# One-core hybrid decoder layer: output strips split two ahead, VectorE's order written out for the first SwiGLU strips, stores on GpSimd's queue, way down in blocks of 3, 4, 4

## The chip, the cores and the metric

The kernel runs on one core of one Trainium2 chip. The metric is device time in microseconds (us), the median of several runs; lower is better. All data is float32 and the matmuls run on float32r operands.

## What is computed

A decoder layer on x of shape (1, 1024, 1024): three mixing branches (gated linear attention, forgetting attention, cross-attention into 256 memory tokens), each projected to 1024 channels, gated and summed, then an output projection with a residual, then a SwiGLU feed-forward layer with another residual. The change touches only the end of it:

```
merged = sum_i gates_i * (y_i @ w_branch[i])
x = x + merged @ w_out
h2 = rmsnorm(x, g_ffn)
x = x + (silu(h2 @ w_ffn_gate) * (h2 @ w_ffn_up)) @ w_ffn_down      # D_FF = 2816
```

## The kernel before, in words

Everything is kept transposed, channels on the 128 partitions and the 1024 tokens along the free axis, in two halves of 512 (`H2`). A float32 operand is split into a high part (ScalarE casts it, L912) and a low part (VectorE subtracts, L913); one product is three matmuls, high·high, high·low, low·high (`mm3`, L844, L846, L848), each 128x128 by 128x512 into one of 8 PSUM banks. The split of a 128x1024 weight strip needs a slot of three rings: `w4` (raw, 6 slots), `h4` and `l4` (high and low, 3 slots each).

- **Output projection** (`out_half`, L923). Two halves of the tokens, 8 strips each; a strip is 24 matmuls. Per strip: load x (L929), load and split a `w_out` strip (L934, L935), the matmuls, the residual add (L940), the store of the new x to DRAM (L941, `x_d`), the square and its sum for the norm. `half_factors` turns the sum into the norm's factors, a broadcast by a matmul with ones (L959), copied to a `w4` tile `rb` (L961). In the second half, after strip 1, eight multiplies (L989) and eight splits (`hop`) make the operands `B11` and `B21` of the first half.
- **SwiGLU in pairs of strips** (L1111 to L1163). The 22 column blocks of gate and up go in 11 pairs; a pair's gate and up are each a 2x2 block product in Strassen-Winograd form, 7 products (`SEQ`, L1000) of 4 steps of `mm3`: 168 matmuls a pair. The weight-side sums are made in `strips` (L1018) from two loads `ra` (L1022) and `rb_` (L1023); the token-side operands (`B11`, `B21`, `T2`, `T1`, `T3`, `B22`, `T4`) are made once, in the first pair (L1129 to L1148), and kept. The first two products need no sums; so PE's order runs those of gate 0, up 0 and gate 1 ahead (their strips are split by `early`, L969), and the other five follow. An intermediate result is read from a PSUM bank while the bank goes on accumulating, by ScalarE (`keep`, L1054) or VectorE (`plus`, L907): the product after next on that bank waits for the read.
- **Stores and sums in passing.** `Pair.store` (L1083) writes the seven operands of the way down to DRAM (`act_d`, L1091). `down_sums` (L1093) loads the down weights of a pair into two `w4` tiles, makes four sums and stores them (`sum_d`, L1104).
- **Way down** (`down`, L1181). Blocks of 3, 3, 3, 2 pairs (`DOWN`, L30); per block four column pairs `jj`, each again 7 products, now of as many steps as the block has pairs. `down_ops` (L1170) loads a pair's seven operands through four `w4` tiles and splits them.

PE's order is the program's (`manual_schedule`, L142). All other engines and the queue of DMA issues on SyncE (SP), on which every DMA is, are put in order by a scheduler that simulates the program's times; once built, each queue is strictly in that order.

Of the kernel before, what the change touches and what calls it, by code (L numbers as in the profile page):

```python
# [12 lines left out]
F32 = mybir.dt.float32  # L13
F32R = mybir.dt.float32r
# [63 lines left out]
def trunk(tc, xT, memT, wT, wmkv, wmq0, wmq1, wgv, wfox, a2, par, cst, wbr, wout, wfg, wfu, wfd, outT):  # L78
# [841 lines left out]
    hops = {}  # L920
    gain = lambda k: pr[:, C_GFFN + k:C_GFFN + k + 1]

    def out_half(h):  # L923

        sl = H2[h]
        ssq = ws.tile([P, 512], F32, tag="l2", bufs=2, name="ssq")
        for j in range(KT):
            x1[j][h] = x = cell("x1")
            nc.sync.dma_start(x, xT[j][:, sl])  # L929
            if h == j == 0:  # L930
                hi, lo = wout0
            else:
                raw = w4()
                nc.sync.dma_start(raw, wout[j])  # L934
                hi, lo = split(h4(), l4(), raw)  # L935
# [33 lines left out]
    def early(src):  # L969
# [3 lines left out]
        return split(ep.tile([P, S], F32R, tag="eh", bufs=2, name="eh"),  # L973
                     ep.tile([P, S], F32R, tag="el", bufs=2, name="el"), raw)

    for ssq in out_half(0):
        if ssq is not None and x1[1][0] is None:
            W0.close()
            E = ExitStack()
            ep = pool(E, "early")  # L980
    fac = half_factors(ssq)
    for j, ssq in enumerate(out_half(1)):
        if j == 0:
            next(fac)
        if j == 1:
            rb = next(fac)
            for k in range(KT):
                x = x1[k][0]
                nc.vector.scalar_tensor_tensor(x, x, gain(k), rb, ALU.mult, ALU.mult)  # L989
                hops["B11" if k < 4 else "B21", k % 4] = hop(hp1, "ha", 8, x)  # L990
        x = x1[j][1]
        nc.scalar.activation(x, x, AF.Copy, scale=gain(j))
        if j > 3:
            sub(x, x, x1[j - 4][1])
    fac = half_factors(ssq)

# [18 lines left out]
                    reads[i](ps)  # L1015
                yield

    def strips(src, first=None):  # L1018

        ra, rb_, sa, sb = w4(), w4(), w4(), w4()  # L1020
        lo_, hi_ = slice(0, 512), slice(512, 1024)
        nc.sync.dma_start(ra, src[:, 0:S])  # L1022
        nc.sync.dma_start(rb_, src[:, S:2 * S])  # L1023
        s2, s1, s3, s4 = sa[:, lo_], sa[:, hi_], sb[:, lo_], sb[:, hi_]
        a = first or split(h4(), l4(), ra)
        add(s1, rb_[:, lo_], rb_[:, hi_])
        sub(s2, s1, ra[:, lo_])
        b = split(h4(), l4(), sa)
        sub(s4, ra[:, hi_], s2)
        sub(s3, ra[:, lo_], rb_[:, lo_])  # L1030
        c = split(h4(), l4(), sb)
        d = split(h2(), l2(), rb_[:, hi_])
        at_ = {"A11": (*a, 0), "A12": (*a, 512), "S2": (*b, 0), "S1": (*b, 512), "S3": (*c, 0), "S4": (*c, 512),
               "A22": (*d, 0)}
# [5 lines left out]
        return get  # L1040

    hB = lambda name, k: hops[name, k]

    class Pair:
# [38 lines left out]
        def store(self, p):  # L1083
            (b11, b12), (b21, b22) = self.u
            t1, t2, t3, t4 = (cell("T") for i in range(4))
            sub(t1, b12, b11)
            sub(t2, b22, t1)
            sub(t3, b22, b12)
            sub(t4, b21, t2)
            for i, t in enumerate((b11, b21, t2, t1, t3, b22, t4)):  # L1090
                nc.sync.dma_start(act_d[p][i], t)  # L1091

    def down_sums(p):  # L1093

        ta, tb = w4(), w4()
        a11, a12, a22, a21 = d = [t[:, s] for t in (ta, tb) for s in H2]
        for o in range(4):
            nc.sync.dma_start(d[o].rearrange("p (j c) -> p j c", c=P), wfd[:, p, :, o, :].rearrange("j p c -> p j c"))
        add(a22, a21, a22)
        sub(a21, a11, a21)  # L1100
        sub(a11, a22, a11)
        sub(a12, a12, a11)
        for o, t in enumerate((a11, a22, a21, a12)):
            nc.sync.dma_start(sum_d[p][:, :, o, :].rearrange("j p c -> p j c"), t.rearrange("p (j c) -> p j c", c=P))  # L1104

    def go(gen, n=99):
        for _ in zip(range(n), gen):
            pass


    pairs = [Pair(), Pair()]  # L1111
    wg0 = strips(wfg[0])
    e1, e2 = early(wfu[0]), early(wfg[1])
    lazy = {}
    late = lambda nm, src, e: lambda name, k: tuple(t[:, (name == "A12") * 512 + k * P:(name == "A12") * 512 + k * P + P]
                                                    for t in e) if name in ("A11", "A12") else lazy[nm](name, k)
    q0, q1, q2 = pairs[0].gate(wg0), pairs[0].up(late("u0", wfu[0], e1)), pairs[1].gate(late("g1", wfg[1], e2))
    go(q0, 4)
    next(fac)
    go(q0, 4)  # L1120
    go(q1, 2)
    rb = next(fac)
    go(q1, 6)
    go(q2, 8)
    E.close()
    BM.close()
    hp2 = pool(root, "h2b")

    for k in range(4):  # L1129
        t3, t2 = x1[k + 4][1], w4()[:, :512]  # L1130
        mul(t3, t3, rb)
        add(t2, t3, x1[k][0])
        hops["T2", k] = hop(hp2, "hb", 20, t2)
        sub(x1[k + 4][0], x1[k + 4][0], t2)
    lazy["u0"] = strips(wfu[0], e1)
    for k in range(4):
        b12, t1 = x1[k][1], x1[k][0]
        mul(b12, b12, rb)
        sub(t1, b12, t1)
        hops["T1", k] = hop(hp2, "hb", 20, t1)  # L1140
    for k in range(4):
        hops["T3", k] = hop(hp2, "hb", 20, x1[k + 4][1])
    for k in range(4):
        b22 = x1[k][1]
        add(b22, x1[k + 4][1], b22)
        hops["B22", k] = hop(hp2, "hb", 20, b22)
    for k in range(4):
        hops["T4", k] = hop(hp2, "hb", 20, x1[k + 4][0])  # L1148
    for i in range(5):
        go(q0, 4)  # L1150
        go(q1, 4)
    pairs[0].store(0)
    lazy["g1"] = strips(wfg[1], e2)
    for p in range(1, NP):
        q = q2 if p == 1 else Pair.gate(pair := Pair(), strips(wfg[p]))
        if p == 1:
# [2 lines left out]
        if p == 4:  # L1159
            down_sums(0)  # L1160
        go(q)
        go(pair.up(strips(wfu[p])))
        pair.store(p)  # L1163


    ORDER = ("B11", "B21", "T2", "T1", "T3", "B22", "T4")
    acc = [[None, None] for j in range(KT)]
    ops = {}

    def down_ops(p):  # L1170

        for i in range(0, 7, 2):
            w = min(2, 7 - i)
            raw = w4()
            nc.sync.dma_start(raw[:, :w * 512].rearrange("p (o c) -> p o c", c=512),
                              act_d[p][i:i + w].rearrange("o p c -> p o c"))
            for o in range(w):
                t = (hp1, "ha", 8) if i == 0 else (hp2, "hb", 20)
                ops[ORDER[i + o], p] = hop(*t, raw[:, o * 512:(o + 1) * 512])

    def down(b, p0, n):  # L1181
        first, last = b == 0, p0 + n == NP
        for q in range(n):
            if (ORDER[0], p0 + q) not in ops:
                down_ops(p0 + q)
        for jj in range(4):
            if jj == 2 and not last:
                down_ops(p0 + n)
# [41 lines left out]
            go(products(get, lambda name, k: ops[name, p0 + k], n, reads))  # L1230

    p0 = 0
    for b, n in enumerate(DOWN):
# [72 lines left out]
```

## Time and profile before

| | us |
|---|---|
| median of 3 runs | 1727.69 (1725.42 to 1728.51) |
| profiled execution, own time | 1728.52 |
| its span, first to last instruction | 1726.7 |
| PE busy | 1672.0 (97%) |
| VectorE (DVE) busy | 992.7 (57%) |
| ScalarE (ACT) busy | 643.4 (37%) |
| GpSimd (POOL) busy | 101.6 (6%) |

The output projection ends at about 1030 us of the span, the SwiGLU pairs at about 1490, the way down at the end. A busy PE is not yet a PE at its rate: each stretch also has a count of matmuls and a granted clock (1.00 is 2.4 GHz, 0.5 is 1.2 GHz), and the three are read together. Engines wait in order: what stands at the head of an engine's queue holds back all behind it.

### The profile page before, as it was taken

To read this page: it belongs to the slowest core of one execution; us is meant where nothing else is said; L and a number is where in the kernel's file an instruction comes from. 1 tells how busy PE (TensorE), PEld (TensorE's weight loads), DVE (VectorE), ACT (ScalarE), POOL (GpSimd) and SP (SyncE) were. 2 spreads that over 40 slices of the span, in tenths; PEclk is the share of its full clock that TensorE was granted. 3 is DMA by queue.
4 is the path that set the end of the run, shared out by engine and by line. 5 is a ranking of instruction groups with operands and counts; after the bars stand their busy time and mean duration, and the time that the engine had idled before them with its cause. 6 is when DMAs were issued, how large, how long until landed. Compare 5 with 4: busy or idle time off the path is not lost.

```text
span 1726.7 us, 21934 instructions
## 1 busy us (share of the span) xinstructions
PE 1672.0 (97%) x8411; PEld 1401.4 (81%) x8411; DVE 992.7 (57%) x1581; ACT 643.4 (37%) x1096; POOL 101.6 (6%) x88
## 2 busy tenths in 40 slices
PE   8999999999999999999999896999999999898999
PEld 7889988878789999988887674877778878686787
DVE  8435554342435565554465468666766665757766
ACT  6334544232224444443123344333333333642421
POOL 2000100000001000000252000000000000000000
PEclk9999999999999999999999997999999999999999
DMA  6441221111231122127546322545545445847633
GB/s 232 134 125 56 68 75 51 62 61 49 62 95 55 62 65 65 50 80 246 195 160 219 115 93 74 182 140 184 162 152 173 141 145 167 264 147 252 209 117 135
DMA packets 152586, 220.79 MB, mean 128 GB/s; under 512 B 11153, under 2 KB 93601, under 8 KB 152481
## 3 DMA queue, kind: packets, MB, share of 16 engines
q1 hardware_dynamic: 152480, 219.39, 39.2%
q8 instruction: 66, 1.08, 0.3%
q14 instruction: 40, 0.32, 0.1%
HBM read 160.30 MB, written 59.05 MB: 127 GB/s over the span
## 4 chain that ended last, share of the span: by engine, by line
PE 85%; DVE 6%; DMA 5%; ACT 2%; issue 1%; SPq 0%; POOL 0%; DVEq 0%; ACTq 0%
PE ps L844 14%; PE ps L848 14%; PE ps L846 14%; PE pt L157 5%; PE pt L159 4%; PE pt L158 4%; PE pm L236 4%; PE pm L238 4%; PE pm L237 4%; PE pm L199 2%; PE pm L203 2%; PE pm L201 2%; DMA w<-in_wfd 2%; DVE hbl L913 1%; DMA w<-in_wfu 1%
## 5 line engine op out<-in xcount | busy, mean ns | idle before, releaser
L844 PE MATMUL ps<-hbh,h 128*128 128x512 f32 x660 | 265.5, 402 | 29.9 <-ACT h L912 12.2
L846 PE MATMUL ps<-hbl,h 128*128 128x512 f32 x660 | 265.0, 402 | 4.3 <-DVE hbl L913 4.3
L848 PE MATMUL ps<-hbh,l 128*128 128x512 f32 x660 | 266.1, 403 | 0.0
L912 ACT CAST h<-w 128x1024 fp32r<-128x1024 f32 (+4 forms) x165 | 141.7, 860 | 329.9 <-PE ps L846 271.8
L913 DVE TENSOR_TENSOR l<-w,h 128x1024 fp32r<-128x1024 f32 (+4 forms) x165 | 162.1, 985 | 60.5 <-ACT h L912 60.2
L844 PEld LDWEIGHTS ps<-hbh,h 128*128 128x128 f32 x660 | 126.7, 192 | 66.4 <-ACT h L912 14.0
L236 PE MATMUL pm<-whi,hh 128*128 128x384 f32 (+2 forms) x512 | 162.3, 317 | 0.0
L238 PE MATMUL pm<-whi,hl 128*128 128x384 f32 (+2 forms) x512 | 159.0, 310 | 0.0
L237 PE MATMUL pm<-wlo,hh 128*128 128x384 f32 (+2 forms) x512 | 158.9, 310 | 0.0
L846 PEld LDWEIGHTS ps<-hbl,h 128*128 128x128 f32 x660 | 126.7, 192 | 35.6 <-DVE hbl L913 4.9
L848 PEld LDWEIGHTS ps<-hbh,l 128*128 128x128 f32 x660 | 126.4, 192 | 30.6 <-DVE l L913 0.8
L157 PE MATMUL pt<-hh,whi 128*128 128x512 f32 x352 | 142.3, 404 | 0.0
L159 PE MATMUL pt<-hh,wlo 128*128 128x512 f32 x352 | 138.1, 392 | 0.0
L158 PE MATMUL pt<-hl,whi 128*128 128x512 f32 x352 | 138.1, 392 | 0.0
L236 PEld LDWEIGHTS pm<-whi,hh 128*128 128x128 f32 x512 | 96.4, 188 | 2.6
L237 PEld LDWEIGHTS pm<-wlo,hh 128*128 128x128 f32 x512 | 96.4, 188 | 2.5
L848 PE MATMUL ps<-hah,l 128*128 128x512 f32 x248 | 96.7, 390 | 1.1 <-DVE l L913 1.1
L846 PE MATMUL ps<-hal,h 128*128 128x512 f32 x248 | 97.1, 392 | 0.0
L844 PE MATMUL ps<-hah,h 128*128 128x512 f32 x248 | 97.0, 391 | 0.0
L238 PEld LDWEIGHTS pm<-whi,hl 128*128 128x128 f32 x512 | 96.3, 188 | 0.0
L189 DVE TENSOR_TENSOR wlo<-raw,whi 128x512 fp32r<-128x512 f32 (+2 forms) x64 | 50.6, 792 | 77.5 <-ACT whi L188 76.9
L907 DVE TENSOR_TENSOR acc<-ps,acc 128x512 f32<-128x512 f32 x96 | 66.2, 690 | 46.0 <-PE ps L848 44.7
(319 smaller groups left out, 3124.3 us busy)
## 6 DMA issues: line engine op xcount, KB each, us to landing
w<-act_d SPq DMA_DIRECT2D x33, 512.0 KB, 4.2
tg<-tg_d SPq DMA_DIRECT2D x24, 512.0 KB, 3.5
w<-in_wfd SPq DMA_DIRECT2D x48, 256.0 KB, 3.3
w<-in_wfg SPq DMA_DIRECT2D x23, 512.0 KB, 4.2
w<-in_wfu SPq DMA_DIRECT2D x23, 512.0 KB, 4.3
raw<-in_wT SPq DMA_DIRECT2D x22, 512.0 KB, 4.2
tg_d<-gz SPq DMA_DIRECT2D x22, 512.0 KB, 2.9
sum_d<-w SPq DMA_DIRECT2D x44, 256.0 KB, 3.0
```

The source lines that it names most:

```text
L157: nc.tensor.matmul(ps, hi[:, ks], hh[k][:, sl], start=k == 0, stop=False)
L158: nc.tensor.matmul(ps, hi[:, ks], hl[k][:, sl], start=False, stop=False)
L159: nc.tensor.matmul(ps, lo[:, ks], hh[k][:, sl], start=False, stop=k == KT - 1)
L236: nc.tensor.matmul(ps[:, :n], hh[k][:, ms], hi, start=k == 0, stop=False)
L237: nc.tensor.matmul(ps[:, :n], hh[k][:, ms], lo, start=False, stop=False)
L238: nc.tensor.matmul(ps[:, :n], hl[k][:, ms], hi, start=False, stop=k == KT - 1)
L844: nc.tensor.matmul(ps, hi, a, start=first, stop=False, skip_group_check=more)
L846: nc.tensor.matmul(ps, hi, b, start=False, stop=False, skip_group_check=more)
L848: nc.tensor.matmul(ps, lo, a, start=False, stop=last, skip_group_check=more)
L907: add = lambda o, a, b: nc.vector.tensor_tensor(o, a, b, ALU.add)
L912: nc.scalar.copy(hi, raw)
L913: nc.vector.tensor_tensor(lo, raw, hi.bitcast(F32), ALU.subtract)
```

## The change

Six edits; the core of the diff:

```diff
-DOWN = (3, 3, 3, 2)
+DOWN = (3, 4, 4)
 # output projection: strips split two ahead; x_d stored from GpSimd's queue
+    wo = {0: wout0}
+    def out_w(i):
+        if i < 2 * KT:
+            raw = w4()
+            nc.sync.dma_start(raw, wout[i % KT])
+            wo[i] = split(h4(), l4(), raw)
+    out_w(1)
...
-            if h == j == 0: hi, lo = wout0
-            else: raw = w4(); nc.sync.dma_start(raw, wout[j]); hi, lo = split(h4(), l4(), raw)
+            out_w(h * KT + j + 2)
+            hi, lo = wo.pop(h * KT + j)
...
-            nc.sync.dma_start(x_d[j][h], x)
+            nc.gpsimd.dma_start(x_d[j][h], x)
 # half_factors: the factors stay in PSUM
-        rb = w4()[:, :512]
-        nc.scalar.copy(rb, ps)
-        yield rb
+        yield ps
 # second half: B11, B21 two a strip; first parts of up 0, gate 1, gate 0 in strips 4, 5, 6
-            for k in range(KT):
+        if 1 <= j <= 4:
+            for k in (2 * j - 2, 2 * j - 1):
                 x = x1[k][0]
                 nc.vector.scalar_tensor_tensor(x, x, gain(k), rb, ALU.mult, ALU.mult)
                 hops["B11" if k < 4 else "B21", k % 4] = hop(hp1, "ha", 8, x)
+        if j == 4: e1 = early(wfu[0])
+        if j == 5: e2 = early(wfg[1])
+        if j == 6: parts_g0 = strip_parts(wfg[0], at_0); next(parts_g0)
...
+    BM.close()                       # before: after E.close(), behind gate 1's first two products
+    hp2 = pool(root, "h2b")          # 16 slots of "hb" (20 before); T4 has a pool of its own, opened after E.close()
 # stores of the way down's operands and sums
-                nc.sync.dma_start(act_d[p][i], t)
+                nc.gpsimd.dma_start(act_d[p][i], t)
...
-            nc.sync.dma_start(sum_d[p]..., t...)
+            nc.gpsimd.dma_start(sum_d[p]..., t...)
 # first pair: VectorE in program order too
+    ve = tc.manual_schedule(engines={mybir.EngineType.DVE})
+    ve.__enter__()
     go(q0, 4); next(fac); go(q0, 4); rb = next(fac)
+    staggered("T2", t2_sum)          # per k: product and sum, cast on ScalarE, then the low part of k - 1
+    go(q1, 8)
+    u0 = strip_parts(wfu[0], at_u, e1); go(u0, 2)          # S2, S1 of up 0
+    staggered("T1", t1_sum)
     go(q2, 8); E.close()
+    go(q0, 4); go(q1, 4); staggered("T3", ...); next(u0)
+    go(q0, 4); go(q1, 4); staggered("B22", b22_sum, lambda: next(u0))
+    go(q0, 4); go(q1, 4); staggered("T4", t4_sum)
+    go(q0, 4); go(q1, 4); g1 = strip_parts(wfg[1], at_g, e2); go(g1, 2)
+    go(q0, 4); go(q1, 4); next(g1); next(g1)
+    ve.__exit__(None, None, None)
 # way down: an operand is loaded into its own low tile and split in place
+    def feed():                      # for each wanted operand, as soon as its ring has a free slot
+                hi = pl.tile(...); lo = pl.tile(...)
+                nc.sync.dma_start(lo.bitcast(F32), act_d[p][ORDER.index(name)])
+                raw.append((x, hi, lo))
+    def need(p0, n): wanted.extend(...); feed()
+    def left(name, n): free[ring(name)[1]] += n; feed()
+    def part(k=99):
+        for x, hi, lo in raw[:k]: ops[x] = split(hi, lo, lo.bitcast(F32))
 # last pair's up product: need(0, 3); after each of its 7 products left(name, 4), after the last three part(3)
 # down: need(next block) at jj == 1; at jj == 3 left(name, n) after each product, part(next n) after the last three;
 #       at jj == 0 part(n) before each product
```

The definitions from `ORDER` to `part` stand twice in the new file, word for word; the second replaces the first. `strip_parts` is `strips` cut into four parts (first split; S2 and S1; the sums S4 and S3; their splits). The number of matmuls is the same.

## Rows read from the trace of the kernel before

**Rows 1.** The page's first part: busy time and share of each engine.
```profile
PE 1672.0 (97%) x8411; PEld 1401.4 (81%) x8411; DVE 992.7 (57%) x1581; ACT 643.4 (37%) x1096; POOL 101.6 (6%) x88
```
**Rows 2.** Stretches: length, busy us (instructions) per engine, granted clock, DMA share, GB/s.
```profile
980.00:1000.00 20.00, 12.27 (x36) 8.64 (x35) 16.61 (x24) 9.97 (x15) 0.00 (x0) 0.74 0.62 223
1040.00:1080.00 40.00, 22.87 (x80) 16.90 (x80) 35.24 (x57) 17.52 (x30) 0.00 (x0) 0.74 0.26 85
1080.00:1160.00 80.00, 80.00 (x346) 64.58 (x345) 51.62 (x71) 26.52 (x38) 0.00 (x0) 1.00 0.52 162
1160.00:1180.00 20.00, 18.07 (x72) 14.26 (x71) 14.99 (x22) 4.90 (x7) 0.00 (x0) 0.91 0.49 167
1200.00:1220.00 20.00, 17.89 (x77) 14.19 (x77) 13.66 (x21) 4.98 (x7) 0.00 (x0) 1.00 0.80 251
1280.00:1300.00 20.00, 19.45 (x84) 15.45 (x83) 15.05 (x22) 5.97 (x8) 0.00 (x0) 1.00 0.54 179
1300.00:1460.00 160.00, 159.88 (x689) 128.92 (x688) 99.56 (x134) 54.01 (x74) 0.00 (x0) 1.00 0.50 156
1480.00:1520.00 40.00, 34.60 (x138) 27.23 (x138) 27.53 (x41) 20.51 (x34) 0.00 (x0) 0.91 0.77 252
1540.00:1600.00 60.00, 54.64 (x225) 42.63 (x224) 46.74 (x72) 24.32 (x40) 0.00 (x0) 0.97 0.78 244
1620.00:1640.00 20.00, 17.15 (x68) 13.42 (x67) 15.26 (x23) 8.00 (x13) 0.00 (x0) 0.91 0.81 242
```
**Rows 3.** What PE waited for from 1040 to 1080 us: total, times, longest.
```profile
PE ps L844 <- ACT h L912: 12.2, 1, 12.2
PE ps L846 <- DVE hbl L913: 4.3, 1, 4.3
```
**Rows 4.** SP's queue in the output projection: start, length, issue, merged count.
```profile
936.18 46.01 SPq L941 DMA_DIRECT2D x_d<-x  x9
982.28 6.64 SPq L934 DMA_DIRECT2D w<-in_wout  x6
```
**Rows 5.** VectorE's timeline, 980 to 992 us.
```profile
983.15 5.38 DVE L989 SCALAR_TENSOR_TENSOR x<-x,pr,w 128x512 f32<-128x512 f32 x8
989.65 1.22 DVE L913 TENSOR_TENSOR l<-w,h 128x1024 fp32r<-128x1024 f32 x1
```
**Rows 6.** The chain of waits in the first pair: start, length, what.
```profile
1036.67 4.91 DVE x L909 x8
...
1061.43 4.82 DVE hbl L913 x8
```
**Rows 7.** Groups of VectorE, then of ScalarE, 920 us on: count, busy, mean ns, idle before.
```profile
L908 DVE TENSOR_TENSOR w<-w,w 128x512 f32<-128x512 f32 x88 | 58.9, 689 | 1.6
...
L912 ACT CAST h<-w 128x1024 fp32r<-128x1024 f32 x79 | 82.9, 1049 | 169.7 <-PE ps L846 150.7 <-issue 9.3 <-DVE w L908 5.4
```
**Rows 8.** One pair, 1150 to 1168 us: SP's queue, then VectorE.
```profile
1154.33 2.58 SPq L1104 DMA_DIRECT2D sum_d<-w  x4
1158.56 0.34 SPq L1023 DMA_DIRECT2D w<-in_wfu  x1
...
1162.72 0.69 DVE L907 TENSOR_TENSOR w<-w 128x512 f32<-128x512 f32 x1 [3.77 <-DMA w<-in_wfu]
1163.33 2.01 DVE L908 TENSOR_TENSOR w<-w,w 128x512 f32<-128x512 f32 x3
...
1166.39 0.68 DVE L907 TENSOR_TENSOR t<-ps,t 128x512 f32<-128x512 f32 x1
```
**Rows 9.** What SP's queue waited for, 920 us on: total, times, longest.
```profile
SPq L1175 <- DVE l L913: 69.6, 23, 7.5
...
SPq L1023 <- DMA sum_d<-w: 8.3, 9, 1.6
```
**Rows 10.** The page's DMA issues: count, KB each, us to landing.
```profile
sum_d<-w SPq DMA_DIRECT2D x44, 256.0 KB, 3.0
```
**Rows 11.** GpSimd's timeline in the norm of the second half.
```profile
1031.17 1.48 POOL L103 TENSOR_TENSOR rcol<-rcol,mhalf 128x4 f32<-128x4 f32 x1 [54.46 <-DVE rcol L102]
```

More of the change, by code (lines that the diff above doesn't have):

```diff
@@ L929, in out_half @@
             nc.sync.dma_start(x, xT[j][:, sl])
[L930 to L935, printed above, removed]
+            out_w(h * KT + j + 2)
+            hi, lo = wo.pop(h * KT + j)
             ps = bank8()
@@ L979, in trunk @@
             E = ExitStack()
-            ep = pool(E, "early")
+            ep = pool(E, "early", side="right")
     fac = half_factors(ssq)
@@ L990, in trunk @@
                 hops["B11" if k < 4 else "B21", k % 4] = hop(hp1, "ha", 8, x)
+        if j == 4:
+            e1 = early(wfu[0])
+        if j == 5:
+            e2 = early(wfg[1])
+        if j == 6:
+            at_0 = {}
+            parts_g0 = strip_parts(wfg[0], at_0)
+            next(parts_g0)
         x = x1[j][1]
@@ L1016, in products, with operand @@
                 yield
[L1018 to L1034, printed above, removed]
+    def operand(at_):
         def get(name, k):
@@ L1040, in strips @@
         return get
+    def strips(src):
+        at_ = {}
+        for _ in strip_parts(src, at_):
+            pass
+        return operand(at_)
     hB = lambda name, k: hops[name, k]
@@ L1103, in down_sums, with need, left, feed @@
         for o, t in enumerate((a11, a22, a21, a12)):
-            nc.sync.dma_start(sum_d[p][:, :, o, :].rearrange("j p c -> p j c"), t.rearrange("p (j c) -> p j c", c=P))
+            nc.gpsimd.dma_start(sum_d[p][:, :, o, :].rearrange("j p c -> p j c"), t.rearrange("p (j c) -> p j c", c=P))
+    ORDER = ("B11", "B21", "T2", "T1", "T3", "B22", "T4")
+    acc = [[None, None] for j in range(KT)]
+    ops = {}
+    wanted = []
+    raw = []
+    free = {"ha": 0, "hb": 0, "hc": 0}
+    def feed():
+        for x in list(wanted):
+            name, p = x
+            pl, tag, n = ring(name)
+            if free[tag]:
+                free[tag] -= 1
+                wanted.remove(x)
+                hi = pl.tile([P, 512], F32R, tag=tag + "h", bufs=n, name=tag + "h")
+                lo = pl.tile([P, 512], F32R, tag=tag + "l", bufs=n, name=tag + "l")
+                nc.sync.dma_start(lo.bitcast(F32), act_d[p][ORDER.index(name)])
+                raw.append((x, hi, lo))
+    def need(p0, n):
+        wanted.extend((name, p) for _, _, name in SEQ for p in range(p0, p0 + n))
+        feed()
+    def left(name, n):
+        free[ring(name)[1]] += n
+        feed()
+    def part(k=99):
+        for x, hi, lo in raw[:k]:
+            ops[x] = split(hi, lo, lo.bitcast(F32))
+        del raw[:k]
+    ORDER = ("B11", "B21", "T2", "T1", "T3", "B22", "T4")
+    acc = [[None, None] for j in range(KT)]
+    ops = {}
+    wanted = []
+    raw = []
+    free = {"ha": 0, "hb": 0, "hc": 0}
+    def feed():
+        for x in list(wanted):
+            name, p = x
+            pl, tag, n = ring(name)
+            if free[tag]:
+                free[tag] -= 1
+                wanted.remove(x)
+                hi = pl.tile([P, 512], F32R, tag=tag + "h", bufs=n, name=tag + "h")
+                lo = pl.tile([P, 512], F32R, tag=tag + "l", bufs=n, name=tag + "l")
+                nc.sync.dma_start(lo.bitcast(F32), act_d[p][ORDER.index(name)])
+                raw.append((x, hi, lo))
+    def need(p0, n):
+        wanted.extend((name, p) for _, _, name in SEQ for p in range(p0, p0 + n))
+        feed()
+    def left(name, n):
+        free[ring(name)[1]] += n
+        feed()
+    def part(k=99):
+        for x, hi, lo in raw[:k]:
+            ops[x] = split(hi, lo, lo.bitcast(F32))
+        del raw[:k]
     def go(gen, n=99):
@@ L1111, in trunk, with raw_lo, staggered, t2_sum @@
     pairs = [Pair(), Pair()]
[L1112 to L1117, printed above, removed]
+    go(parts_g0)
+    at_u, at_g = ({"A11": (*e, 0), "A12": (*e, 512)} for e in (e1, e2))
+    q0, q1, q2 = pairs[0].gate(operand(at_0)), pairs[0].up(operand(at_u)), pairs[1].gate(operand(at_g))
+    def raw_lo(name, k, raw):
+        pl, tag, n = ring(name)
+        hi = pl.tile([P, 512], F32R, tag=tag + "h", bufs=n, name=tag + "h")
+        lo = pl.tile([P, 512], F32R, tag=tag + "l", bufs=n, name=tag + "l")
+        nc.scalar.copy(hi, raw)
+        hops[name, k] = hi, lo
+        return lambda: sub(lo, raw, hi.bitcast(F32))
+    def staggered(name, work, between=None):
+        last = None
+        for k in range(4):
+            raw = work(k)
+            lo = raw_lo(name, k, raw)
+            if last:
+                last()
+            last = lo
+            if between and k == 1:
+                between()
+        last()
+    def t2_sum(k):
+        t3, t2 = x1[k + 4][1], t2s[k]
+        mul(t3, t3, rb)
+        add(t2, t3, x1[k][0])
+        return t2
+    def t1_sum(k):
+        b12, t1 = x1[k][1], x1[k][0]
+        mul(b12, b12, rb)
+        sub(t1, b12, t1)
+        return t1
+    def b22_sum(k):
+        add(x1[k][1], x1[k + 4][1], x1[k][1])
+        return x1[k][1]
+    def t4_sum(k):
+        sub(x1[k + 4][0], x1[k + 4][0], t2s[k])
+        return x1[k + 4][0]
+    ve = tc.manual_schedule(engines={mybir.EngineType.DVE})
+    ve.__enter__()
     go(q0, 4)
@@ L1120, in trunk @@
     go(q0, 4)
-    go(q1, 2)
     rb = next(fac)
-    go(q1, 6)
+    t2s = [t[:, s] for t in (w4(), w4()) for s in H2]
+    ring = lambda name: RING.get(name, (hp2, "hb", 16))
+    RING = {"B11": (hp1, "ha", 8), "B21": (hp1, "ha", 8)}
+    staggered("T2", t2_sum)
+    go(q1, 8)
+    u0 = strip_parts(wfu[0], at_u, e1)
+    go(u0, 2)
+    staggered("T1", t1_sum)
     go(q2, 8)
     E.close()
[L1126 to L1151, printed above, removed]
+    hp3 = pool(root, "h2c")
+    RING["T4"] = (hp3, "hc", 4)
+    go(q0, 4)
+    go(q1, 4)
+    staggered("T3", lambda k: x1[k + 4][1])
+    next(u0)
+    go(q0, 4)
+    go(q1, 4)
+    staggered("B22", b22_sum, lambda: next(u0))
+    go(q0, 4)
+    go(q1, 4)
+    staggered("T4", t4_sum)
+    go(q0, 4)
+    go(q1, 4)
+    g1 = strip_parts(wfg[1], at_g, e2)
+    go(g1, 2)
+    go(q0, 4)
+    go(q1, 4)
+    next(g1)
+    next(g1)
+    ve.__exit__(None, None, None)
     pairs[0].store(0)
-    lazy["g1"] = strips(wfg[1], e2)
     for p in range(1, NP):
@@ L1161, in trunk @@
         go(q)
-        go(pair.up(strips(wfu[p])))
-        pair.store(p)
[L1166 to L1179, printed above, removed]
+        q = pair.up(strips(wfu[p]))
+        if p == NP - 1:
+            need(0, DOWN[0])
+            for i, (_, _, name) in enumerate(SEQ):
+                go(q, 4)
+                left(name, 4)
+                if i > 3:
+                    part(DOWN[0])
+        go(q)
+        pair.store(p)
     def down(b, p0, n):
[L1182 to L1185, printed above, removed]
+        last = p0 + n == NP
         for jj in range(4):
-            if jj == 2 and not last:
-                down_ops(p0 + n)
+            if jj == 1 and not last:
+                need(p0 + n, DOWN[b + 1])
             three = lambda t: t[:, :n * 2 * P].rearrange("p (n c) -> p n c", c=2 * P)
@@ L1229, in down @@
                         add(acc[j][h], acc[j][h], x[:, s])
-            go(products(get, lambda name, k: ops[name, p0 + k], n, reads))
+            q = products(get, lambda name, k: ops[name, p0 + k], n, reads)
+            for i, (_, _, name) in enumerate(SEQ):
+                if jj == 0:
+                    part(n)
+                go(q, n)
+                if jj == 3 and not last:
+                    left(name, n)
+                if i > 3 and jj == 3 and not last:
+                    part(DOWN[b + 1])
+            go(q)
     p0 = 0
```

20 lines of the change are left out of this document (added).

## The prediction

> **What bounds the kernel now.** I read the page's busy times first: PE is busy for 1672.0 of 1726.7 us [rows 1], so only PE's gaps and the stretches in which it ran slowly can be won. The table of stretches was read next, its count of matmuls above all. Undisturbed, PE does 346 matmuls in 80 us, 4.33 per us, so a step (three matmuls) takes 0.69 us, an output strip (24) 5.5 us and a pair of SwiGLU strips (168) 38.8 us [rows 2]. Dividing what a stretch falls short of that rate by 4.33 gives its loss, the fall of the clock included (0.74 means that half of the stretch ran at 1.2 GHz): 980 to 1000 us 11.7; 1040 to 1080 us 21.5; 1160, 1200 and 1280 us 3.4, 2.2 and 0.6; 1480 to 1520 us 8.1; 1540 to 1600 us 8.0; 1620 us 4.3 [rows 2]. Together 59.8 us. The waits of PE, the chain and SP's queue then say what ended each.
>
> **The change, part by part.**
>
> *Output strips two ahead, stores off SP's queue.* From 936 to 982 us SP's queue is taken up by nine stores `x_d`, each at the queue's head until its sum is made; six loads of `w_out` strips come behind them, at 982.28 [rows 4]. Then VectorE runs all eight multiplies L989 (5.38 us) before the next strip's low part at 989.65 [rows 5], and PE stands. With the change the loads have no store in front of them, and a strip's split is asked for 11 us before PE needs it. VectorE's work must still fit. Strips 1 to 4 of the second half each take 1.22 (low part) + 2 x 0.69 (residual, square sum) + 2 x (0.67 + 0.69) = 5.3 us of the 5.5 [rows 5, 7]; all seven strips, with the four subtractions of strips 4 to 7 (2.8), the three early splits (3.7) and gate 0's next sums and split (2.6), take about 36 of 38.8 us. Full, but ahead of PE. I leave 0.5 us and take 11.2 of the 11.7. If VectorE falls behind instead, up to the whole 11.7 stays.
>
> The Trainium skill, "DMA: Bandwidth & Descriptors", section "Issuing engines are not separate DMA queues", says that issuing DMAs from several engines saves only the sequencer's issue time. By that rule this move is worth next to nothing (it becomes a rival below); the row shows another cost, 46 us of waiting at the head of one queue, which the rule leaves out.
>
> *First pair, VectorE in program order.* PE stood once for 12.2 us and once for 4.3 [rows 3]: VectorE first did eight multiplies (4.91 us) and all sums and low parts of later products (another run of 4.82 us ends at 1066.2) before the sums of up 0 [rows 6]. In the new order I count from the factors in PSUM (T = 0), VectorE's 512-wide operations at 0.61 us in a run (4.91 / 8), a 1024-wide low part at 1.22, ScalarE's cast of it at 1.05 [rows 5 to 7]. PE has 16 steps as cover, to 11.1 us. T2: 12 operations, to 7.3. The two reads of up 0: 8.7. S2, S1 of up 0: two sums, cast, low part, to 12.2, while PE does gate 0's S2 product to 13.9 and up 0's to 16.6: no wait. T1: 12 operations to 19.5, its low parts done at 15.2, 17.1, 18.9, 19.5, while PE wants them at 16.6, 17.3, 18.0, 18.7: it ends 0.9 late, and up 0's product at 23.1. T3, the sums for S3 and S4, half of B22 and the low part of up 0's S3 reach 26.9 when PE wants that at 25.9 (its high parts come earlier): 0.6. B22 ends at 30.7, in time but for tenths. Three reads, T4's eight operations to 37.7: PE 0.9 late. Three reads and gate 1's S2 to 43.3, PE there at 41.2: 1.7. Sum 4.1 us of waiting. For the clock, and for ScalarE's part that I counted only in two places, I double it: 8 us are left of 21.5, 13.5 won. Bounds: 4 left if all overlaps so, 21.5 if a load or a cast holds VectorE's now rigid order. Keeping `rb` in PSUM drops one copy on ScalarE; the multiplies then read PSUM, which I take at the same 0.61 (the sums from PSUM into SBUF take 0.68 [rows 8]).
>
> *Stores of `act_d` and `sum_d` on GpSimd's queue.* This is where a cost can come in. In a pair, `sum_d` is issued at 1154.33, the load of up's second half follows only at 1158.56, VectorE waits 3.77 us for it, makes four sums (2.7) and a low part (1.2), and the read `t` that PE needs to go on comes at 1166.39 [rows 8]. SP's load waited for a landing of `sum_d` nine times [rows 9]: its `w4` slot is the one that the stores give back, so in nine pairs a later landing goes through to VectorE's read. PE's own loss from it is 6.2 us now (three stretches, [rows 2]). No row shows a store issued by GpSimd. Below: it lands as on SP, 3.0 us after issue [rows 10], nothing lost; or the order comes out so that the reads go first, and the 6.2 us are won. Above: each of the two stores that free the slot takes GpSimd as long as its last small operation there, 1.48 us [rows 11], against 1.3 for two issues on SP (2.58 / 2): 2 x 1.48 - 1.3 = 1.7 us later, nine times, 15 us. The 3.0 us landing is the nearest row; I take 0.7 us later, and half of the nine pairs passing it on: 3 us lost. GpSimd itself is idle there (0.00 busy [rows 2]); eleven stores a pair fit while one takes under 3.5 us. `x_d`'s store also holds back ScalarE's scaling of x (L992), which has two strips of slack now.
>
> The same page, section "Specifications", gives a first byte after about 1 us on GpSimd's path and 0.6 us on SP's. By that the landing would be an estimated 0.4 us later and the loss nearer 2 than 3 us.
>
> *Way down.* Before, its operands go through `w4`: SP waited 69.6 us in 23 places for such a slot [rows 9], and the first products lost 8.1 us [rows 2]. Now an operand needs no `w4` slot and the loads of block 0 start during the last up product, as its rings come free; nine of 21 operands are split by then, the others at three per product. Block 0's first column pair asks VectorE for 12 x 0.69 + 3 x 0.95 (768 of 1024 columns of 1.22, rounded up) + 4 x 0.69 = 14 us of 21 steps, 14.5: just covered. I leave 2 us, 6.1 won. The block boundaries cost 8.0 + 4.3. Three become two, and a read now has a product of 4 x 0.69 = 2.8 us to hide in where it had 2.1. But block 1's first column pair holds 16 operand splits, its own strips (3 x 1.22 + 0.69), seven reads and four additions of x: 27 x 0.61 + 4.4 = 20.9 us against 28 steps, 19.3. And 28 loads of 256 KB per boundary, 7.3 MB, take about 29 us at the 252 GB/s of the way down's first stretch, while PE gives 19 us for a column pair and as much again before the last is wanted. I leave 5 us (bounds 1 and 12.3): 7.3 won. Fewer evictions (84 instead of 112) lie beside PE and count nothing.
>
> **Sum.** 11.2 + 13.5 - 3 + 6.1 + 7.3 = 35.1 us off the profiled execution's 1728.52 gives 1693.4. The median of the runs shown is 0.8 us below that execution: about 1692 us.
>
> **The rivals.**
> 1. *All of it works.* 0.5 + 4 + 0 + 1 + 1 us are left of 59.8: 1728.5 - 53 = 1675. For it: no wait lies outside the places that the edits touch. Against: VectorE at 97% of some stretches, by my own count.
> 2. *Half of it.* Stores land 2 us later (9 x 2 = 18 us more loss), or the rigid order is held by one load (first pair wins 2 instead of 13.5), or the queue move is worth only issue time, as the rule above has it, and the 11.2 us stay: each costs 10 to 18 us of my sum, 1703 to 1711, for all three cases. For it: the read has little slack in three of the nine pairs; against: the 46 us in rows 4.
> 3. *Slower: the landing of `sum_d` decides.* The one mechanism: stores of many short rows take GpSimd so long that the slot comes back late by d, in nine pairs PE waits for d, and each such wait also halves the clock for a while (the 1160 us stretch: 1.93 us idle, 3.4 lost, so 1.5 on top). Elsewhere 38 us are won, so it decides from 9 x (d + 1.5) = 38, d = 2.7 us. At d = 5 it is 9 x 6.5 = 58 us: 1749. For it: three stretches show the chain already closed, and the price of a store there is unknown. Against: twice 1.48 us is the longest that a row suggests.
> 4. *No change.* Gains and the landing cancel, d near 2.7.
>
> **How the numbers follow.** My forecast, 1682 to 1703 around 1692, gets 0.52; rival 1 0.13; rival 2 0.23; rival 3 0.08; rival 4 0.04. The range takes the forecast, most of rival 2 and a part of rival 1: 1677 to 1714. About 0.2% (3.5 us) is what a measurement of this kernel can tell from no change; faster by more than that is forecast and rivals 1 and 2, 0.88; within it 0.04; slower 0.08.
>
> **What would show it.** In the changed kernel's table of stretches the output projection's second half should run at 4.3 matmuls per us with the clock at 1.00 and VectorE nearly full. The first pair should show several waits of about 1 us on low parts of T1, T4 and gate 1's S2, no single one of 12. In the SwiGLU pairs the time from `sum_d`'s issue to the load behind it is the number to read: 4.2 us now (1154.33 to 1158.56); 5 is my case, 7 or more rival 3, with VectorE's wait for `in_wfu` grown by as much. The way down should have no wait of PE at its start above 2 us, and short ones after block 1 begins. I am wrong if PE's loss before 1000 us or in the first pair is unchanged, or if a pair regularly takes more than 40 us.

## The result, and the profile after

| | before | changed |
|---|---|---|
| median of 4 runs, us | 1726.56 (1723.29 to 1728.51) | 1705.57 (1703.6 to 1710.81) |
| ratio to before | 1 | 0.9885 (95%: 0.9858 to 0.9913) |
| profiled execution, own time | 1728.52 | 1705.77 |
| its span | 1726.7 | 1703.9 |

The change makes the kernel 21 us faster. The forecast was 1692 us, 35 us faster: the sign and the range (1677 to 1714) hold, and 14 us of the expected gain are missing.

The page of the changed kernel, first part: busy time and share of each engine, and the count of instructions.

```profile
PE 1662.8 (98%) x8411; PEld 1393.4 (82%) x8411; DVE 972.0 (57%) x1537; ACT 639.1 (38%) x1078; POOL 185.8 (11%) x225
```

Beside [rows 1], PE is busy 9 us less although it does the same 8411 matmuls, and GpSimd, which now issues the stores, 84 us more. The table of stretches of the changed kernel (columns as in [rows 2]) says where the rest went.

```profile
980.00:1000.00 20.00, 20.00 (x85) 15.78 (x84) 19.01 (x28) 10.81 (x17) 1.68 (x3) 1.00 0.19 69
1040.00:1080.00 40.00, 35.10 (x143) 25.77 (x142) 36.66 (x57) 19.14 (x31) 4.77 (x8) 1.00 0.39 128
1084.00:1465.00 381.00, 366.95 (x1557) 294.38 (x1556) 236.70 (x320) 124.26 (x173) 64.88 (x104) 0.99 0.50 160
1470.00:1510.00 40.00, 35.72 (x147) 28.51 (x146) 27.90 (x44) 20.29 (x34) 3.24 (x6) 0.96 0.65 226
1530.00:1640.00 110.00, 107.60 (x459) 85.38 (x458) 84.67 (x122) 50.93 (x75) 0.00 (x0) 1.00 0.75 251
```

At the prediction's rate of 4.33 matmuls per us, 85 matmuls in 20 us lose 0.4 us where 11.7 were lost; 143 in 40 us lose 7.0 where 21.5 were; the start of the way down loses 6.1 where 8.1 were, its block boundaries 4.0 where 12.3 were. The third row is the new one: over the pairs from 1084 to 1465 us PE does 1557 matmuls in 381 us, 21 us short, where the pairs of before lost 6.2 in three stretches.

A second reading does without a rate. PE's order of matmuls is the program's, so I compare the time at which its n-th matmul starts in two profiled executions; the lead over before at the end of each part, and its growth over the part, are (worked out from the traces):

| lead over before, us | output projection | first pair | pairs | way down | growth in these four |
|---|---|---|---|---|---|
| changed kernel | 10.5 | 26.0 | 11.6 | 23.2 | +11.5, +15.4, -14.3, +11.6 |
| `sum_d` back on SP | 9.5 | 21.9 | 22.3 | 31.9 | +10.5, +12.4, +0.4, +9.5 |
| before with stores on GpSimd | -0.9 | -1.9 | -16.6 | -15.9 | +0.6, -1.0, -14.7, +0.7 |
| VectorE's order free | 10.3 | 15.2 | -0.3 | 9.3 | +12.1, +4.9, -15.5, +9.5 |
| blocks of 3, 3, 3, 2 | 11.0 | 23.5 | 11.7 | 10.9 | +11.7, +12.5, -11.8, -0.7 |
| best version (last experiment) | 9.6 | 23.6 | 22.8 | 36.8 | +10.0, +13.9, -0.8, +14.0 |

(The lead early in the output projection, between -0.4 and -1.8 us in these runs, is the start that the first growth counts from; the pairs end with the last matmul before the way down's first.) One execution of the same code differs from the next by some 3 us in a part: the first pair's order is the same in the first, second, fifth and sixth row. The pairs give back more than half of what the first two parts win.

### The profile page after: what moved, and what is told of

Read it like the earlier page. It is cut to its first block, busy times and chain, and to the rows that moved or that the text cites. A ratio compares the mean times of both kernels' runs of the same rounds, so it can differ in the third digit from the quotient of the medians.

```text
span 1703.9 us, 21967 instructions
## 1 busy us (share of the span) xinstructions
PE 1662.8 (98%) x8411; PEld 1393.4 (82%) x8411; DVE 972.0 (57%) x1537; ACT 639.1 (38%) x1078; POOL 185.8 (11%) x225
## 4 chain that ended last, share of the span: by engine, by line
PE 79%; DMA 8%; DVE 7%; ACT 2%; issue 2%; SPq 0%; POOL 0%; DVEq 0%; POOLq 0%; ACTq 0%
PE ps L844 12%; PE ps L846 12%; PE ps L848 12%; PE pt L157 5%; PE pt L158 4%; PE pt L159 4%; PE pm L236 4%; PE pm L237 4%; PE pm L238 4%; DMA w<-in_wfu 2%; PE pm L199 2%; DMA w<-in_wfd 2%; DVE l L913 2%; PE pm L203 2%; PE pm L201 2%
## 5 line engine op out<-in xcount | busy, mean ns | idle before, releaser
L912 ACT CAST h<-w 128x1024 fp32r<-128x1024 f32 (+3 forms) x149 | 138.8, 931 | 312.1 <-PE ps L846 274.6
L844 PE MATMUL ps<-hbh,h 128*128 128x512 f32 x528 | 209.5, 397 | 8.2 <-ACT acc L1342 5.2
L848 PE MATMUL ps<-hbh,l 128*128 128x512 f32 x528 | 210.6, 399 | 1.4 <-DVE l L913 1.4
L846 PE MATMUL ps<-hbl,h 128*128 128x512 f32 x528 | 209.2, 396 | 1.8 <-DVE hbl L908 1.8
L913 DVE TENSOR_TENSOR l<-w,h 128x1024 fp32r<-128x1024 f32 (+3 forms) x149 | 160.0, 1076 | 55.3 <-ACT h L912 54.5
L844 PEld LDWEIGHTS ps<-hbh,h 128*128 128x128 f32 x528 | 99.6, 189 | 34.9 <-ACT acc L1342 6.0
L846 PEld LDWEIGHTS ps<-hbl,h 128*128 128x128 f32 x528 | 99.5, 189 | 27.2 <-DVE hbl L908 2.9
L848 PEld LDWEIGHTS ps<-hbh,l 128*128 128x128 f32 x528 | 99.6, 189 | 25.8 <-DVE l L913 2.3
L907 DVE TENSOR_TENSOR acc<-ps,acc 128x512 f32<-128x512 f32 x68 | 47.1, 692 | 63.3 <-PE ps L848 63.3
```

What stands on the lines that cost most here:

```text
L844: nc.tensor.matmul(ps, hi, a, start=first, stop=False, skip_group_check=more)
L846: nc.tensor.matmul(ps, hi, b, start=False, stop=False, skip_group_check=more)
L848: nc.tensor.matmul(ps, lo, a, start=False, stop=last, skip_group_check=more)
L912: nc.scalar.copy(hi, raw)
L913: nc.vector.tensor_tensor(lo, raw, hi.bitcast(F32), ALU.subtract)
```

## The experiments

Each ratio is to runs of before on the same chip, with its 95% interval.

**1. `sum_on_sp`: the stores of the sums back on SP's queue.**

```diff
-            nc.gpsimd.dma_start(sum_d[p]..., t...)
+            nc.sync.dma_start(sum_d[p]..., t...)
```

> The changed kernel with the stores of sum_d alone back on SP's queue. Theory A (in the pairs the store of sum_d on GpSimd's queue, and the load of up's second half that runs beside it, are later than on SP): the load's landing falls from a median of 5.0 us to about 4.3, PE's waits on the read t in the pairs from 14 us to about 6, and the time from 1705.6 to about 1694 us. Rival B (the pairs lose because the whole front now runs ahead and the loads meet other traffic, whichever queue issues the stores): same waits, 1703 to 1708 us. Rival C (act_d is what crowds the load): little change here, and the gain comes with act_d on SP instead.

Measured: 1696.33 us, ratio 0.9809 (0.9794 to 0.9824), against 0.9885 for the whole change. So this one edit of the change costs some 13 us by the ratios (0.76% of 1728; 9 us between the two times, which are from different chips), and the pairs are where: they win 0.4 us instead of losing 14.3. What PE waited for from 1084 to 1465 us (total, times, longest): the changed kernel first, then this one.

```profile
PE ps L844 <- DVE t L907: 14.1, 8, 3.4
```

```profile
PE ps L844 <- DVE t L907: 4.9, 5, 1.4
```

Before, the same wait took 4.6 us in 3 places. One pair shows the chain. The changed kernel from 1130 to 1145 us, GpSimd, SP and VectorE in turn (start, length, what, count, idle time before it and its releaser):

```profile
1130.01 2.99 POOL L1130 DMA_DIRECT2D sum_d<-w  x4 [17.81 <-DVE w L907]
...
1134.13 0.34 SPq L985 DMA_DIRECT2D w<-in_wfu  x1
...
1139.64 0.69 DVE L907 TENSOR_TENSOR w<-w 128x512 f32<-128x512 f32 x1 [5.28 <-DMA w<-in_wfu]
...
1142.18 1.22 DVE L913 TENSOR_TENSOR l<-w,h 128x1024 fp32r<-128x1024 f32 x1
1143.32 0.69 DVE L907 TENSOR_TENSOR t<-ps,t 128x512 f32<-128x512 f32 x1
```

The same pair with `sum_d` on SP:

```profile
1132.61 2.54 SPq L1130 DMA_DIRECT2D sum_d<-w  x4
1135.89 0.34 SPq L985 DMA_DIRECT2D w<-in_wfu  x1
...
1140.31 0.69 DVE L907 TENSOR_TENSOR w<-w 128x512 f32<-128x512 f32 x1 [3.09 <-DMA w<-in_wfu]
```

Read from the load's issue to VectorE's first sum: 5.51 us (1134.13 to 1139.64) against 4.42 (1135.89 to 1140.31). The load that follows the stores is itself slower. The DMA groups of 1084 to 1465 us (count, KB each, median us from issue to landing), changed kernel and then this one:

```profile
sum_d<-w POOLq DMA_DIRECT2D x41, 256.0 KB, 3.6
w<-in_wfu SPq DMA_DIRECT2D x18, 512.0 KB, 5.1
```

```profile
sum_d<-w SPq DMA_DIRECT2D x41, 256.0 KB, 3.2
w<-in_wfu SPq DMA_DIRECT2D x18, 512.0 KB, 4.7
```

**2. `before_pool_stores`: the kernel before, with `act_d` and `sum_d` on GpSimd's queue.** The converse: this edit of the change alone.

```diff
-                nc.sync.dma_start(act_d[p][i], t)
+                nc.gpsimd.dma_start(act_d[p][i], t)
...
-            nc.sync.dma_start(sum_d[p]..., t...)
+            nc.gpsimd.dma_start(sum_d[p]..., t...)
```

> The kernel before with act_d and sum_d on GpSimd's queue and nothing else changed. Theory A: the pairs lose what they lost in the changed kernel, 10 to 14 us: 1736 to 1741 us. Rival B (it is not the queue): 1726 us within 3.

Measured: 1744.02 us, ratio 1.0086 (1.0071 to 1.0101): 14 us slower, and the table of leads puts all of it into the pairs. PE's waits there:

```profile
PE ps L844 <- DVE t L907: 16.6, 9, 3.3
```

So the loss needs nothing else of the change.

**3. `act_on_sp`: only `act_d` back on SP.**

```diff
-                nc.gpsimd.dma_start(act_d[p][i], t)
+                nc.sync.dma_start(act_d[p][i], t)
```

> The changed kernel with the stores of act_d alone back on SP's queue. Theory A: sum_d is what counts, so about 1705 us, or some us slower, since SP's loads again stand behind stores that wait for VectorE (SP waited 33.4 us on those before). Rival C (act_d on GpSimd crowds the load): 1694 to 1698 us.

Measured: 1708.52 us, ratio 0.9876 (0.986 to 0.9893), the pairs still giving back 15.3 us. The stores of `act_d` show no part in the loss.

**4. `sum_half_pool`: two of the four sums on each queue.** The two that free the slot of the load behind (o = 1, 2) stay on GpSimd, the others go on SP.

```diff
-            nc.gpsimd.dma_start(sum_d[p]..., t...)
+            (nc.gpsimd if o in (1, 2) else nc.sync).dma_start(sum_d[p]..., t...)
```

> The changed kernel with the two sum_d stores that free the w4 slot (a22, a21) on GpSimd's queue and the other two (a11, a12) on SP's. It parts the two pieces of the loss in a pair. If the load of up's second half is slowed by the other two stores while they are still moving on GpSimd's queue, its landing falls from 5.4 to about 4.4 us with the slot freed as late as before (5.0 us behind the sum), and the time is about 1699 us. If it is slowed by the first two or by act_d, it stays at 5.3 and the time at 1703 to 1707 us.

Measured: 1704.96 us, ratio 0.9851 (0.9834 to 0.9869). Over the seven regular pairs (those with one set of sums, in which the load comes right behind the stores in every run compared) the load takes a median of 4.63 us from issue to landing, against 5.36 in the changed kernel and 4.52 with all on SP; but its slot came free 5.62 us after the first sum's start, later than the changed kernel's 4.99, and the time can't be told from the changed kernel's (0.9885, its interval overlaps). The load is less slowed with half the stores on GpSimd; the run as a whole is inconclusive, and why stores there slow it stays open. The record has one difference that no run tests by itself: GpSimd's stores go in fewer, longer packets. The packets of the second DMA queue (queue, packets, MB, share) from 1084 to 1465 us, changed kernel and then `sum_on_sp`:

```profile
q0 software_dynamic: 8400, 27.53, 22.2%
```

```profile
q0 software_dynamic: 5120, 16.78, 11.3%
```

The 41 stores between them had 80 packets each there, 64 of 4096 bytes and 16 short ones; on SP's queue the same store goes in 512 of 512 bytes.

**5. `up_first`: `sum_d` on SP, and the loads of up's strip issued ahead of the sums.**

```diff
+        ups = strip_loads(wfu[p])             # the two loads, ahead of down_sums
...
-        q = pair.up(strips(wfu[p]))
+        q = pair.up(strips(wfu[p], ups))
```

> The changed kernel with sum_d on SP's queue and, in each pair, up's two loads asked for ahead of the down weights' sums, so that they no longer wait for the slot that sum_d's stores give back. Theory (the chain sum_d's landing, load, VectorE's sums, read is what PE waits for in the pairs): the waits on the read t go below 2 us in all, some 5 to 8 us under sum_d on SP alone (ratio to before 0.976 to 0.978). Rival (the slot is short whoever asks first: now the next gate's load waits): ratio 0.980 to 0.983 as with sum_d on SP alone.

Measured: 1695.76 us, ratio 0.9795 (0.9779 to 0.981). The intervals of this run and of experiment 1 overlap: no gain that the time shows. PE's waits of the pairs fall only from 4.9 to 4.3 us (2.6 once on VectorE's read, 1.7 in two places on ScalarE's), not below the 2 that the theory asked for.

**6. `dve_free`: the first pair without VectorE's written order.** The two lines that open `ve` and the one that closes it are left out; the reordered program stays.

> The changed kernel without VectorE's written order in the first pair (the pieces stand in the same program order, the scheduler may move them). Theory: the order itself is what removed PE's 12.2 and 4.3 us waits, so a wait of several us comes back between 1040 and 1070 us and the first pair loses 5 to 15 us: 1711 to 1721 us. Rival: the earlier place for T2 and T1 (free of gate 1's operands) and the cut of the strips into parts suffice, and the scheduler finds as good an order: 1705.6 within 3 us.

Measured: 1719.49 us, ratio 0.9936 (0.992 to 0.9953), some 9 us slower than the change. PE's waits from 1020 to 1080 us, the changed kernel first, then this one:

```profile
PE ps L846 <- DVE hbl L908: 1.8, 2, 1.0
PE ps L848 <- DVE l L913: 1.4, 2, 0.9
PE ps L844 <- ACT h L912: 1.3, 1, 1.3
PE ps L846 <- DVE hcl L908: 0.2, 1, 0.2
```

```profile
PE ps L848 <- DVE l L913: 7.8, 1, 7.8
PE ps L846 <- DVE hbl L908: 2.5, 2, 1.4
PE ps L844 <- ACT h L912: 1.0, 1, 1.0
```

One long wait is back, and it lies in a stretch at 1.2 GHz (columns as in [rows 2]):

```profile
1038.00:1058.00 20.00, 10.35 (x23) 7.08 (x24) 20.00 (x34) 9.58 (x17) 0.60 (x1) 0.50 0.28 92
```

VectorE is busy throughout: it isn't short of work, it does other work first. The first pair wins 4.9 us where it wins 12.4 to 15.4 with the order, so the order is worth 7.5 to 10.5 us; what the other 4.9 come from was not separated.

**7. Four runs on the output projection.** `x_on_sp` puts the store of x back on SP; `no_ahead` splits a strip when it is due; `no_ahead_x_on_sp` does both; `mult_once` does all eight multiplies in one strip again and keeps queue and lookahead.

```diff
-            nc.gpsimd.dma_start(x_d[j][h], x)      # x_on_sp
+            nc.sync.dma_start(x_d[j][h], x)
-    out_w(1)                                       # no_ahead
-            out_w(h * KT + j + 2)
+            if h * KT + j: out_w(h * KT + j)
-        if 1 <= j <= 4:                            # mult_once
-            for k in (2 * j - 2, 2 * j - 1):
+        if j == 1:
+            for k in range(KT):
```

> The changed kernel with the stores x_d of the output projection back on SP's queue, strips still asked for two ahead. Theory A (the nine stores at the head of SP's queue were the wait, 46 us of it): SP holds the strips' loads again and PE waits for a strip around 985 us, up to the 11.2 us that were lost there: 1709 to 1717 us. Rival (asking two ahead is what does it, the queue is worth only issue time): 1705.6 within 3 us.

> The changed kernel with each output strip asked for when its turn comes, not two ahead; x_d stays on GpSimd's queue and the eight multiplies stay spread over four strips. Theory (asking ahead is what removes the wait at 985 us): up to 11.2 us come back, 1712 to 1717 us. Rival (spreading the multiplies or the free queue is enough): 1705.6 within 3 us.

> The changed kernel with both undone, strips asked for when their turn comes and x_d on SP's queue; the multiplies stay spread. Theory D: no wait at 985 us, ratio 0.986 to 0.989. Rival E: the wait of about 10 us is back, ratio about 0.994.

> The changed kernel with all eight multiplies (and splits) of B11 and B21 in one go behind strip 1 of the second half, as before; strips asked for two ahead and x_d on GpSimd's queue as changed. Undoing either of those two alone brought no wait back. Theory D (the spread of the multiplies is what removed the wait at 985 us): about 10 us come back there, ratio to before about 0.994. Rival E (asking ahead or the free queue each suffice, so nothing comes back while one of them stands): ratio 0.986 to 0.989, as the changed kernel.

Measured: 1708.43 us, ratio 0.9879 (0.9864 to 0.9893); 1707.22, 0.9868 (0.985 to 0.9886); 1709.16, 0.9885 (0.9871 to 0.99); 1705.32, 0.9857 (0.9833 to 0.988). The growth in the output projection is 10.6, 11.8, 11.4 and 11.4 us: none of them brings the wait back. My theory, that the stores of x at the head of SP's queue held the loads, falls. With `no_ahead_x_on_sp`, SP's queue has store and load in turn and PE doesn't wait:

```profile
976.44 0.33 SPq L946 DMA_DIRECT2D x_d<-x  x1
977.84 0.33 SPq L928 DMA_DIRECT2D w<-in_wout  x1
```

And `mult_once` shows that spreading the multiplies isn't needed either, as long as queue and lookahead stay changed. VectorE still runs all eight together, 5.35 us, before the next low part, as in [rows 5], and PE doesn't wait:

```profile
983.12 5.35 DVE L1016 SCALAR_TENSOR_TENSOR x<-x,pr,ps 128x512 f32<-128x512 f32 x8 [0.17 <-PE ps L965]
988.39 1.22 DVE L913 TENSOR_TENSOR l<-w,h 128x1024 fp32r<-128x1024 f32 x1
```

**8. `down_3332`: the way down in blocks of 3, 3, 3, 2.**

```diff
-DOWN = (3, 4, 4)
+DOWN = (3, 3, 3, 2)
```

> The changed kernel with the way down in blocks of 3, 3, 3, 2 pairs, operands still loaded and split in place. Theory (no w4 slots for the operands is the larger part of the way down's 11 us, longer products the smaller): 2 to 5 us of short waits on reads come back, ratio 0.988 to 0.991. Rival (the longer products do it): 7 to 10 us come back, ratio 0.992 to 0.994.

Measured: 1714.35 us, ratio 0.9918 (0.9899 to 0.9937). PE's waits from 1460 us on, the changed kernel first, then this one:

```profile
PE ps L844 <- ACT acc L1342: 5.2, 2, 4.3
PE ps L844 <- DVE acc L907: 1.5, 2, 0.8
```

```profile
PE ps L844 <- DVE acc L907: 6.1, 6, 1.9
PE ps L844 <- ACT acc L1342: 5.9, 2, 5.5
```

The short waits on VectorE's read of a bank, which the longer product covers, are back; the one at the start is there in both. By the table the way down's growth goes from +11.6 to -0.7 us, nearly all of it behind the start (+9.4 to -0.5); but this profiled execution took 3.6 us more than its median, and the two ratios are only 5.7 us apart with overlapping intervals, between the two expectations. So the blocks are worth some 6 us by the times and up to 12 by the profile. What splitting the operands in place is worth was not measured by itself.

**9. `up_first_act`: experiment 5, and ScalarE in the program's order in the first column pair of the way down.**

```diff
+            am = tc.manual_schedule(engines={mybir.EngineType.Activation}) if b == jj == 0 else ExitStack()
+            am.__enter__()
...
+            am.__exit__(None, None, None)
```

> sum_d on SP's queue, up's loads asked for first, and ScalarE in program order in the first column pair of the way down, so that its first read of a bank no longer stands behind casts that wait for the T4 operands' loads. Theory (that order is PE's 4 to 5 us wait at the start of the way down, with the clock's fall 6 to 7): ratio about 0.976. Rival (the loads are late there whatever the order, and the wait moves to the next read or product): ratio 0.979 as without it.

Measured: 1691.54 us (1687.34 to 1692.48), ratio 0.9779 (0.9761 to 0.9798): the best version, ahead of before and of the changed kernel. It was made for what the changed kernel's start of the way down shows, in the chain of waits (start, length, what):

```profile
1475.86 6.92 DMA hcl<-act_d
...
1482.81 0.62 ACT hch L912
1483.43 0.49 ACT acc L1342
1483.96 0.80 PE ps L844
```

ScalarE's read of the first bank (L1342), which PE's third product waits for, stands in ScalarE's queue behind casts of `hcl`, whose load takes 6.92 us to land. With the program's order that wait is gone, and those of the way down are short:

```profile
PE ps L844 <- ACT acc L1348: 3.5, 3, 1.6
PE ps L844 <- ACT hah L912: 1.1, 1, 1.1
PE ps L844 <- DVE acc L907: 0.7, 1, 0.7
```

The way down's growth is 14.0 us where `up_first` had 9.5. As a time, that step alone (0.9795 to 0.9779) is within the intervals.

## Why the prediction was right or wrong

**Output projection: size right, reason wrong.** 11.2 us were forecast, 11.5 came; that the sizes agree is luck. The reason given, nine stores at the head of SP's queue and too little lookahead, isn't what the gain hangs on: neither edit is needed, nor both, nor, with both in place, the spread of the multiplies. Two edits in this part were undone in no run: the early splits of the first SwiGLU strips, which stand in the program behind the place of the wait, and the norm's factors `rb`, which stay in PSUM and no longer take a `w4` slot. The latter fits the rows of before: the loads that come late are issued at 982.28 [rows 4], as ScalarE writes `rb` into its `w4` tile:

```profile
982.41 0.57 ACT L961 COPY w<-ps 128x512 f32<-128x512 f32 x1
```

The tile is taken in program order behind strip 9's, and the raw strips after it come in order behind it: the six late loads are strips 10 to 15, all that stand behind `rb` in the ring and none before it. The last of the six waited for the multiplies that read `rb`, as it would if it took the slot that `rb` gave back (SP's queue of before, 920 us on):

```profile
SPq L934 <- DVE x L989: 3.9, 1, 3.9
```

The prediction costed that edit as one copy less. This is an inference: `rb` was not put back by itself, and queue, lookahead and spread were not undone all at once. The Trainium skill, "DMA: Bandwidth & Descriptors", section "Issuing engines are not separate DMA queues", which gives a second issuing engine no more than saved issue time, agrees with `x_on_sp`: 0.9879 against 0.9885. For the stores of `sum_d` it doesn't hold: their move costs 14 us (experiment 2).

**First pair: right.** 13.5 us were forecast from a count of VectorE's work product by product, and 15.4 came. The four waits counted (0.9, 0.6, 0.9 and 1.7 us on T1, up 0's S3, T4 and gate 1's S2) are there, as 1.8, 0.9, 0.2 and 1.9 us, 4.7 in all against 4.1 counted. Doubled for the clock, 8 us were to be left of the stretch's 21.5; 7.0 were. The 2 us above the forecast are luck: the clock was granted at 1.00 from 1040 to 1080 us, but with the same waits at 0.91 in `sum_on_sp`, whose first pair won 12.4.

**Stores and pairs: the chain right, a link left out.** This term was -3 us and measured -14.3; it is 11 of the 12 us missing between the profiled executions. The step had two factors. The landing, taken as 0.7 us later, is: over the seven regular pairs, from the start of the first of the four sums to the landing of the store that frees the slot, the median is 4.21 us before and 4.99 changed. (The Trainium skill, "DMA: Bandwidth & Descriptors", section "Specifications", had given an estimated 0.4 us by its first-byte figures; of the 0.8, some 0.5 lie between issue and landing, near it, and 0.3 before the issue.) What was left out, put at nothing without a reason, is the load behind it: up's second half took 4.24 us before and 5.36 now. The data come 1.8 us later instead of 0.7 (8.66 to 10.45 us from the same start), and eight of nine pairs pass it on instead of half. Rival 3's chain is the one that decided, at a delay of 1.8 us, below the 2.7 at which it would have eaten the whole gain. The clock that it charged on top, 1.5 us a wait, cost some 5 us in all: the granted clock was 0.57 from 1142 to 1150 us and 0.66 from 1309 to 1314, and six of the eight waits left it at 1.00; with the 14.1 us of waits that is 19 of the 21 us lost.

Of the signs that the prediction named, the time from the first store's issue to the load's read 4.1 us in the pair shown (1130.01 to 1134.13), where 4.2 had stood before and 5 was my case: it begins and ends in the wrong place, since the issue itself had come later and the loss lies behind the load's issue. VectorE's wait for the load did grow, from 3.77 us in [rows 8] to 5.28. And by its own test, no pair regularly over 40 us, the prediction is wrong in this part: the eight pairs with the wait take 40.7 to 42.5 us each, where six of those eight took 39.0 to 39.7 before. One row was misread, too: the 2.58 us of [rows 8], from which 1.3 us for two issues on SP were taken, hold waits for the next sum; an issue there takes 0.37 us.

**Way down: 13.4 forecast, 11.6 came, divided otherwise.** The start was to give 6.1 us and gave 2.0 by the rate. A wait of 1.1 us in the first product went; the long one is still there: PE stood before the third product for 4.3 us in before and for 4.3 in the changed kernel, each time for ScalarE's first read of a bank. What PE waited for in before, from 1480 to 1640 us, and the end of the chain there:

```profile
PE ps L844 <- ACT acc L1214: 4.3, 1, 4.3
...
PE ps L848 <- DVE l L913: 1.1, 1, 1.1
```

```profile
1492.30 3.66 DMA w<-in_wfd
1495.98 0.51 ACT h L912
1496.49 0.49 ACT acc L1214
1497.03 0.79 PE ps L844
```

L1214 is the changed kernel's L1342. In before the read stood behind the cast of a down strip that came late, now it stands behind a cast of `hcl`; the change swapped what is in front and left the wait. The prediction, which took the 69.6 us that SP waited for `w4` slots as the cause and counted VectorE's work alone, didn't look at ScalarE's order, though the row was there; "no wait above 2 us at its start" was one of its signs, and it failed. The boundaries were to give 7.3 and gave 8.3. That longer products cover the read is what the waits on VectorE say: 1.5 us in 2 places, and 6.1 in 6 with the shorter blocks of `down_3332`.

**Sum.** 11.5 + 15.4 - 14.3 + 11.6 = 24.2; the first 1.0 us and the last 0.4 are lost elsewhere, and the span is 22.8 us shorter. Against the 35.1 of the forecast: pairs -11.3, way down -1.8, first pair +1.9, output projection +0.3. The range held, but of the five terms only the first pair's and the boundaries' came near their size for the reason given.

## What to carry to other kernels

A store on another queue is priced by who waits for its landing and by what else is on its way at that time: where its slot is next filled by a load that the bottleneck waits for, measure the store's landing and that load's duration, both. A wait that comes with a full queue isn't shown to be caused by it: ask which buffer ring the late instruction takes its slot from, and in what order. Where an engine's work fits by count, its order still has to be read: one read behind one late load held PE for 4.3 us, in both kernels.

## What the runs showed of the hardware

- Issuing a 256 KB store of `sum_d` takes GpSimd 0.75 us (2.99 / 4, one behind the other), SP 0.37 (the 2.54 us of its four hold waits for the next sum); landing is 3.6 against 3.2 us at the median. The same store goes in 64 packets of 4096 bytes from GpSimd and in 512 of 512 bytes from SP, short ones aside.
- A load of 512 KB on SP that runs beside such stores takes 5.36 us instead of 4.52 in otherwise the same kernel; with half of the stores moved it is 4.63. Why was not settled.
- In `dve_free` the clock was at 1.2 GHz from 1038 us on, for 20 us; it fell as PE had two waits of 1.4 us or less and before the long one of 7.8. The changed kernel, with two waits of 1.0 us or less from 1041 to 1044 us, kept 2.4 GHz; `sum_on_sp`, with the same two, fell to 1.2 GHz for 3.4 us behind them. Of the eight waits in the changed kernel's pairs (0.8 to 3.4 us) two came with a fall, of 3.4 and 1.8 us; one of 2.2 us did not. So the length of a wait alone didn't tell whether the clock fell.
